# Splitting shared weights once: the first sequence stores the two-part weights, the second loads them

## The chip, the cores and the metric

One core of a Trainium2 chip runs the whole program. The metric is the time of one execution on the device in microseconds (us), lower is better. The engines named below are PE (matrix products), DVE and ACT (elementwise work), POOL, and SP, which here only issues transfers between main memory and the on-chip buffers.

## The reference

Two independent sequences, `prompt` and `sample`, of 1024 tokens by 1024 features, pass through the same encoder layer with the same weights. Cut to its core:

```python
h = rmsnorm(x, norm_g) * (1 + scale) + shift            # scale, shift, gate from the conditioning vector
a_b, a_c, a_x, a_z, q, k, v, b_z, lr_f, lr_b, m_a, m_b = split(h @ w_in)
y_a = (a_b * depthwise_conv(a_c * a_x) * silu(a_z)) @ w_a_out
o   = gated_linear_attention(q, k, v, forward) + gated_linear_attention(q, k, v, backward)
y_b = (rmsnorm_heads(o) * silu(b_z)) @ w_b_out
merged = sigmoid(m_a) * y_a + sigmoid(m_b) * y_b
y = rmsnorm(x + gate * (merged @ w_out), final_norm_g)
```

All arithmetic is float32. A product of two float32 matrices is made on PE as three products of parts: each operand is split into a rounded `hi` (an ACT cast) and a remainder `lo` (a DVE subtraction), and hi·hi, hi·lo and lo·hi are summed.

## The kernel before

The weight matrices lie in main memory as 112 tiles of 128 by 1024 floats (512 KB each). The program goes once through the stages for sequence 0 and then through the same stages for sequence 1: `projections` (most of `h @ w_in`), `mixers` (attention of four heads, one after the other, with products of the remaining projections and of `w_a_out` laid between its steps), and `merge` (`w_b_out`, `merged`). A `final` stage makes the product with `w_out` for both.

There are two kinds of products. The projections use a scheme of seven products for a 2 by 2 block of tiles (`fast`, `stationary`). Their weight operands are already made in parts only once: sequence 0 writes them to `kept_d` (L190) and sequence 1 loads them from there (`loaded`, L226 and L231). The other kind are the plain products, which take one weight tile through `load_w` (L126): two transfers of 256 KB bring the halves of a tile into `raw` buffers (L117), ACT makes `hi` (L122), DVE makes `lo` (L123), both into a `w` buffer. There are 6 `raw` buffers and 4 `w` buffers (`NW`), so the `w` buffers hold two tiles. A plain tile of weights takes 48 matmuls of 512 columns: 8 slices of the features, two halves of the tokens, three products of parts.

From weight tile `W_Q` (32) to the last of `W_B` (87) each sequence takes 28 tiles through `load_w`: in `mixers`, `gates` takes 4 of `W_Q` and `W_K` and 8 of `W_MA`; `first_out` takes 8 of `W_A`; `merge` takes 8 of `W_B`. The last two tiles of `gates`, the first two and the last two of `first_out` go as a pair through `group` (L340), which holds all four `w` buffers and four accumulators; the others go one at a time through `halves` (L328). `mixers` draws dense steps from these two generators after each step of the attention: the loop keeps a debt `owed`, to which each attention step adds 20 dense steps per head in proportion to its length.

While the last pair of `gates` runs, `reload` (L1053) brings the convolution's output in from `ta_d` for `first_out`: 16 transfers through the same 6 `raw` buffers, each split on ACT and DVE into the operand `b`. The results of that pair are taken out of the accumulators by ACT (`sg`, L764). The attention's levels copy keys on ACT (`km`, L931), multiply on PE (L903) and update Q and K on DVE (L944, L947).

[...]

Of the kernel before, what the change touches and what calls it, by code (L numbers as in the profile page):

```python
# [11 lines left out]
F32 = mybir.dt.float32  # L12
F32R = mybir.dt.float32r
# [4 lines left out]
P = 128  # L18
# [4 lines left out]
HALF = 512  # L23
# [9 lines left out]
W_AB, W_AC, W_AX, W_AZ, W_Q, W_K, W_V, W_BZ, W_MA, W_MB, W_A, W_B, W_ADA, W_GATE = (  # L33
    0, 8, 16, 24, 32, 36, 40, 48, 56, 64, 72, 80, 88, 104)
NTILES = 112
NBIG, NSMALL, NW, NRAW = 18, 6, 4, 6
# [21 lines left out]
def encoder_kernel(ctx, tc, x_p, x_s, x_t, weights, w_lr, w_gate, w_out, vectors, b_gate, final_norm_g, masks, y_p, y_s):  # L58
    nc = tc.nc
# [5 lines left out]
    sb = ctx.enter_context(tc.tile_pool(name="sb", bufs=1))  # L65
# [3 lines left out]
    dram = ctx.enter_context(tc.tile_pool(name="dram", bufs=1, space=bass.MemoryType.DRAM))  # L69
# [30 lines left out]
    mk = const.tile([P, len(MASKED), P], U8, name="mk")  # L100

    q_d, k_d, v_d, z_d, t_d = ([dram.tile([NH, P, 2, L], F32, name=f"{n}_d{s}") for s in range(2)] for n in "qkvzt")
    kept_d = dram.tile([36, 7, P, 2 * HALF], F32, name="kept_d")
    g_d = [dram.tile([2 * KT, P, L], F32, name=f"g_d{s}") for s in range(2)]
    m1_d = [dram.tile([KT, P, L], F32, name=f"m1_d{s}") for s in range(2)]
# [8 lines left out]
    def staged(src, queue=lambda load: None):  # L114

        raw = sb.tile([P, HALF], F32, name="raw", tag="raw", bufs=NRAW)
        queue(nc.sync.dma_start(out=raw, in_=src))  # L117
        return raw

    def split(hi, lo, raw, engine):  # L120

        high = nc.scalar.copy(out=hi, in_=raw)  # L122
        engine.tensor_sub(out=lo, in0=raw, in1=hi.bitcast(F32))  # L123
        return high

    def load_w(i, w=None, **kw):  # L126

        with tc.high_priority(offset=30):
            parts = []
            raws = [staged(weights[i][:, half * HALF:(half + 1) * HALF], **kw) for half in range(2)]  # L130
            for half, raw in enumerate(raws):
                t = sb.tile([P, 2, 4, P], F32R, name="w", tag="w", bufs=NW) if w is None else w[:, half]
                split(t[:, 0], t[:, 1], raw.rearrange("p (k c) -> p k c", c=P), nc.vector)
                parts.append(t)
        return lambda k: (parts[k // 4][:, 0, k % 4, :], parts[k // 4][:, 1, k % 4, :])

    def product(out, terms, first=True, last=True):
# [190 lines left out]
    def halves(i, use, act, w=None):  # L328

        w = w or load_w(i)  # L330
        for t in range(2):
            sl = slice(t * HALF, (t + 1) * HALF)
            ps = dense_ps()
            for ks in (range(KT // 2), range(KT // 2, KT)):
                mm3(ps, w, lambda k: act(k, sl), ks=ks, first=(ks[0] == 0), last=(ks[0] > 0))
                if ks[0]:
                    use(ps, sl)
                yield

    def group(items, act):  # L340


        ws = [load_w(i) for i, _ in items]
        pss = [[dense_ps(), dense_ps()] for _ in items]
        for k in range(KT):
            for w, ps in zip(ws, pss):
                for t in range(2):
                    mm3(ps[t], w, lambda k: act(k, slice(t * HALF, (t + 1) * HALF)), ks=[k], first=(k == 0), last=(k == KT - 1))
            yield
        for (_, use), ps in zip(items, pss):  # L350
            for t in range(2):
                use(ps[t], slice(t * HALF, (t + 1) * HALF))
# [63 lines left out]
    def start(mv):  # L416
# [51 lines left out]
        def weights_of(i):  # L468
            first.append(load_w((W_AC, W_AX, W_AZ)[i], w=big("wf", F32R, (P, 2, 2, 4, P)) if i == 2 else None, queue=queue))
# [748 lines left out]
```

## Time and profile before

| | |
|---|---|
| runs of the kernel | 2373.42 us median of 3 (2373.26 to 2377.82) |
| profiled execution, its own time | 2377.87 us |
| profiled execution, span of the trace | 2376.0 us |
| mean granted clock of PE | 0.987 |
| busy: PE, DVE, ACT | 2301.9, 1424.6, 1008.8 us |

The profiled execution's time is 1.87 us above its span and 4.45 us above the median of the runs. Sequence 0 has its mixers from about 666 to 1060 us and its merge to 1167; sequence 1 has its projections from 1167 to 1727, its mixers to 2110 and its merge to 2195.

### The profile page before, as it was taken

To read this page: it belongs to the slowest core of one execution; us is meant where nothing else is said; L and a number is where in the kernel's file an instruction comes from. 1 tells how busy PE (TensorE), PEld (TensorE's weight loads), DVE (VectorE), ACT (ScalarE), POOL (GpSimd) and SP (SyncE) were. 2 spreads that over 40 slices of the span, in tenths; PEclk is the share of its full clock that TensorE was granted. 3 is DMA by queue.
4 is the path that set the end of the run, shared out by engine and by line. 5 is a ranking of instruction groups with operands and counts; after the bars stand their busy time and mean duration, and the time that the engine had idled before them with its cause. 6 is when DMAs were issued, how large, how long until landed. Compare 5 with 4: busy or idle time off the path is not lost.

```text
span 2376.0 us, 29248 instructions
## 1 busy us (share of the span) xinstructions
PE 2301.9 (97%) x10897; PEld 1883.3 (79%) x10897; DVE 1424.6 (60%) x2021; ACT 1008.8 (42%) x1655; POOL 34.3 (1%) x72
## 2 busy tenths in 40 slices
PE   7999999999999989999999999999999989999998
PEld 3688887887888868878788888888778878888887
DVE  4676676666576878868622332344476876965443
ACT  4443443666655546443421112555145544442221
POOL 0000000000000000000000000000000000000000
PEclk8999999999999999999999999999999999999999
DMA  6267767888863245557366667787853244478431
GB/s 234 71 245 282 268 252 279 314 298 302 308 235 110 99 146 201 211 184 245 113 202 212 212 201 230 256 277 269 306 187 113 101 150 169 160 246 300 154 124 62
DMA packets 189902, 494.63 MB, mean 208 GB/s; under 512 B 18912, under 2 KB 45632, under 8 KB 185664
## 3 DMA queue, kind: packets, MB, share of 16 engines
q1 hardware_dynamic: 166960, 405.98, 49.8%
q10 hardware_dynamic: 22800, 86.78, 9.4%
q8 instruction: 86, 1.41, 0.2%
q14 instruction: 56, 0.46, 0.1%
HBM read 294.90 MB, written 197.79 MB: 207 GB/s over the span
## 4 chain that ended last, share of the span: by engine, by line
PE 83%; DMA 7%; DVE 6%; ACT 2%; issue 1%; POOL 1%; SPq 0%; POOLq 0%; DVEq 0%; ACTq 0%
PE ps L141 9%; PE ps L143 9%; PE ps L142 9%; PE pl L277 8%; PE pl L278 8%; PE pl L279 8%; PE ps L278 6%; PE ps L279 6%; PE ps L277 6%; PE pl L903 3%; DMA raw<-in_weights_dram 2%; DMA qk<-q_d 2%; PE pm L141 1%; PE pm L142 1%; PE pm L143 1%
## 5 line engine op out<-in xcount | busy, mean ns | idle before, releaser
L123 DVE TENSOR_TENSOR w<-raw,w 128x512 fp32r<-128x512 f32 x298 | 202.2, 686 | 100.1 <-ACT w L122 99.1
L122 ACT CAST w<-raw 128x512 fp32r<-128x512 f32 x298 | 183.3, 621 | 161.7 <-PE ps L143 51.5
L277 PE MATMUL pl<-th,w 128*128 128x512 f32 x584 | 228.1, 391 | 1.1 <-ACT keep L282 1.1
L278 PE MATMUL pl<-tl,w 128*128 128x512 f32 x584 | 227.9, 390 | 0.0
L279 PE MATMUL pl<-th,w 128*128 128x512 f32 x584 | 227.6, 390 | 0.0
L141 PE MATMUL ps<-b,w 128*128 128x512 f32 x512 | 202.8, 396 | 0.4 <-ACT w L122 0.3
L142 PE MATMUL ps<-b,w 128*128 128x512 f32 x512 | 201.8, 394 | 0.2 <-DVE b L123 0.2
L143 PE MATMUL ps<-b,w 128*128 128x512 f32 x512 | 201.0, 393 | 0.0
L141 PE MATMUL ps<-hi,w 128*128 128x512 f32 x432 | 173.5, 402 | 1.7 <-ACT hi L390 1.7
L143 PE MATMUL ps<-hi,w 128*128 128x512 f32 x432 | 171.2, 397 | 1.5 <-DVE w L123 1.5
L142 PE MATMUL ps<-lo,w 128*128 128x512 f32 x432 | 170.7, 395 | 0.7 <-DVE lo L391 0.7
L282 ACT COPY keep<-pl 128x512 f32<-128x512 f32 x116 | 67.7, 584 | 242.2 <-PE pl L279 242.1
L278 PE MATMUL ps<-lo,w 128*128 128x512 f32 x352 | 138.2, 393 | 0.4 <-DVE lo L123 0.4
L279 PE MATMUL ps<-hi,w 128*128 128x512 f32 x352 | 137.8, 391 | 0.4 <-DVE w L123 0.4
L277 PE MATMUL ps<-hi,w 128*128 128x512 f32 x352 | 137.7, 391 | 0.3 <-ACT hi L122 0.3
L277 PEld LDWEIGHTS pl<-th,w 128*128 128x128 f32 x584 | 110.0, 188 | 24.9 <-ACT keep L282 1.7
L278 PEld LDWEIGHTS pl<-tl,w 128*128 128x128 f32 x584 | 109.9, 188 | 23.0
L279 PEld LDWEIGHTS pl<-th,w 128*128 128x128 f32 x584 | 109.8, 188 | 22.9
L903 PE MATMUL pl<-Q,km 128*128 128x128 f32 x768 | 101.8, 287 | 19.4 <-ACT km L931 14.5
L903 PEld LDWEIGHTS pl<-Q,km 128*128 128x128 f32 x768 | 95.3, 198 | 31.5 <-ACT km L931 20.1
L141 PEld LDWEIGHTS ps<-b,w 128*128 128x128 f32 x512 | 97.0, 189 | 19.3 <-ACT w L122 0.7
L142 PEld LDWEIGHTS ps<-b,w 128*128 128x128 f32 x512 | 96.9, 189 | 19.0 <-DVE b L123 1.0
(287 smaller groups left out, 5043.7 us busy)
## 6 DMA issues: line engine op xcount, KB each, us to landing
kept_d<-w SPq DMA_DIRECT2D x196, 512.0 KB, 4.1
raw<-in_weights_dram SPq DMA_DIRECT2D x256, 256.0 KB, 4.3
w<-kept_d SPq DMA_DIRECT2D x112, 512.0 KB, 3.4
wk<-kept_d SPq DMA_DIRECT2D x168, 256.0 KB, 3.1
g<-g_d SPq DMA_DIRECT2D x32, 512.0 KB, 4.6
araw<-in_weights_dram SPq DMA_DIRECT2D x16, 512.0 KB, 3.7
ta_d<-u ACTq DMA_DIRECT2D x16, 512.0 KB, 3.5
v_d<-single ACTq DMA_DIRECT2D x16, 512.0 KB, 5.2
```

What stands on the lines that cost most here:

```text
L122: high = nc.scalar.copy(out=hi, in_=raw)
L123: engine.tensor_sub(out=lo, in0=raw, in1=hi.bitcast(F32))
L141: nc.tensor.matmul(out, ahi, bhi, start=(first and i == 0), stop=False)
L142: nc.tensor.matmul(out, ahi, blo, start=False, stop=False)
L143: nc.tensor.matmul(out, alo, bhi, start=False, stop=(last and i == n - 1))
L277: nc.tensor.matmul(ps, whi[:, cs], mhi, start=(first and k == 0), stop=False, skip_group_check=True)
L278: nc.tensor.matmul(ps, whi[:, cs], mlo, start=False, stop=False, skip_group_check=True)
L279: nc.tensor.matmul(ps, wlo[:, cs], mhi, start=False, stop=(k == 3), skip_group_check=True)
L282: nc.scalar.copy(out=job[i, "keep"], in_=ps)
L903: nc.tensor.matmul(pl[:, j * P:(j + 1) * P], km[:, c * P:(c + 1) * P], qm(c), start=True, stop=True)
```

## The change

For every tile from `W_Q` on, the first sequence's `load_w` also writes each half, split into its two parts, to a new memory tensor `plain_d` (512 KB per half), and notes it in `kept_w`. The second sequence's `load_w` finds the tile there and loads both halves straight into `w` buffers, without `raw`, without the cast and without the subtraction. This branch stands ahead of the `high_priority` block.

```diff
+    plain_d = dram.tile([W_ADA - W_Q, 2, P, 2 * HALF], F32, name="plain_d")
+    kept_w = {}
     kept_d = dram.tile([36, 7, P, 2 * HALF], F32, name="kept_d")
...
     def load_w(i, w=None, **kw):
 
+        if i in kept_w:
+            parts = []
+            for half in range(2):
+                t = sb.tile([P, 2, 4, P], F32R, name="w", tag="w", bufs=NW)
+                nc.sync.dma_start(out=t.bitcast(F32).rearrange("p a k c -> p (a k c)"), in_=kept_w[i][half])
+                parts.append(t)
+            return lambda k: (parts[k // 4][:, 0, k % 4, :], parts[k // 4][:, 1, k % 4, :])
         with tc.high_priority(offset=30):
             parts = []
             raws = [staged(weights[i][:, half * HALF:(half + 1) * HALF], **kw) for half in range(2)]
@@ -132,6 +141,11 @@
                 t = sb.tile([P, 2, 4, P], F32R, name="w", tag="w", bufs=NW) if w is None else w[:, half]
                 split(t[:, 0], t[:, 1], raw.rearrange("p (k c) -> p k c", c=P), nc.vector)
                 parts.append(t)
+                if i >= W_Q:
+
+                    nc.sync.dma_start(out=plain_d[i - W_Q, half], in_=t.bitcast(F32).rearrange("p a k c -> p (a k c)"))
+            if i >= W_Q:
+                kept_w[i] = plain_d[i - W_Q]
```

## Rows read from the trace of the kernel before

**Rows 1.** Page, costliest groups: form, xcount | busy us, mean ns | idle before.
```profile
L123 DVE TENSOR_TENSOR w<-raw,w 128x512 fp32r<-128x512 f32 x298 | 202.2, 686 | 100.1 <-ACT w L122 99.1
L122 ACT CAST w<-raw 128x512 fp32r<-128x512 f32 x298 | 183.3, 621 | 161.7 <-PE ps L143 51.5
```
**Rows 2.** Windows by stage: length, busy and count of each engine, clock, DMA share, GB/s.
```profile
111.00:666.00 555.00, 548.51 (x2401) 450.48 (x2400) 360.67 (x493) 284.97 (x410) 0.00 (x0) 0.99 0.77 281
666.00:1060.00 394.00, 371.25 (x2049) 313.12 (x2048) 301.88 (x462) 201.61 (x403) 9.64 (x16) 0.98 0.46 161
1060.00:1167.00 107.00, 105.08 (x451) 84.98 (x449) 81.98 (x111) 45.53 (x60) 0.00 (x0) 0.98 0.60 203
1167.00:1727.00 560.00, 553.46 (x2430) 454.84 (x2429) 197.07 (x227) 178.65 (x216) 0.00 (x0) 1.00 0.70 236
1727.00:2110.00 383.00, 367.44 (x2041) 308.92 (x2039) 292.74 (x447) 189.09 (x381) 9.68 (x16) 0.99 0.42 151
2110.00:2195.00 85.00, 83.99 (x374) 69.41 (x375) 46.16 (x65) 23.15 (x34) 0.00 (x0) 1.00 0.87 296
```
**Rows 3.** PE's waits in sequence 1's mixers (1727 to 2110): us, times, longest.
```profile
PE pl L903 <- ACT km L931: 6.7, 3, 5.0
PE pm L1046 <- DVE ot L1038: 3.3, 7, 0.5
PE pl L370 <- ACT Xh L122: 2.7, 2, 2.5
PE pl L903 <- ACT w L122: 2.1, 1, 2.1
PE ps L141 <- ACT w L122: 0.3, 1, 0.3
```
**Rows 4.** Timeline of PE, 1942 to 1960: start, us, instruction, [idle before].
```profile
1942.44 0.39 PE L143 MATMUL ps<-hi,w 128*128 128x512 f32 x1
1944.06 2.05 PE L903 MATMUL pl<-Q,km 128*128 128x128 f32 x16 [1.24 <-ACT km L931]
1951.10 3.78 PE L903 MATMUL pl<-Q,km 128*128 128x128 f32 x16 [4.99 <-ACT km L931]
1957.01 2.02 PE L903 MATMUL pl<-Q,km 128*128 128x128 f32 x16 [2.12 <-ACT w L122]
1959.16 0.50 PE L141 MATMUL ps<-b,w 128*128 128x512 f32 x1
```
**Rows 5.** Timeline of ACT, 1955 to 1960.
```profile
1955.32 1.04 ACT L931 COPY km<-K 128x1024 f32<-128x1024 f32 x1
1956.26 0.61 ACT L122 CAST w<-raw 128x512 fp32r<-128x512 f32 x1
1957.99 0.62 ACT L122 CAST w<-raw 128x512 fp32r<-128x512 f32 x1 [1.12 <-DMA raw<-in_weights_dram]
1958.52 1.56 ACT L764 ACTIVATE sg<-ps 128x512 f32<-128x512 f32 x3
```
**Rows 6.** Timeline of DVE, the update of Q before the third level's matmuls.
```profile
1955.65 1.21 DVE L944 TENSOR_TENSOR Q<-Q,T 128x1024 f32<-128x1024 f32 x1
```
**Rows 7.** Windows of 4 us: before and inside that stretch, and of sequence 0's.
```profile
1936.00:1940.00 4.00, 4.00 (x27) 3.59 (x26) 4.00 (x7) 1.80 (x3) 0.00 (x0) 1.00 0.21 62
1948.00:1952.00 4.00, 0.90 (x4) 0.90 (x5) 4.00 (x8) 2.32 (x4) 0.00 (x0) 0.58 0.24 86
...
896.00:900.00 4.00, 4.00 (x20) 3.30 (x19) 2.75 (x5) 1.05 (x1) 0.00 (x0) 1.00 1.05 436
```
**Rows 8.** Page, DMA issues: xcount, KB each, median us from issue to landing.
```profile
kept_d<-w SPq DMA_DIRECT2D x196, 512.0 KB, 4.1
raw<-in_weights_dram SPq DMA_DIRECT2D x256, 256.0 KB, 4.3
w<-kept_d SPq DMA_DIRECT2D x112, 512.0 KB, 3.4
```
**Rows 9.** SP's own waits over the whole span, first of the list: us, times, longest.
```profile
SPq L117 <- DVE w L123: 462.3, 96, 20.1
SPq L190 <- DVE w L123: 209.7, 109, 20.1
```
**Rows 10.** Chain that ended last, 860 to 990 (sequence 0): start, us, link.
```profile
900.17 6.53 DMA raw<-in_x_t_dram
932.94 4.24 DMA raw<-in_x_t_dram
```

## Prediction

> **What bounds the kernel now.** I read the windows by stage first [rows 2]. In each stage PE is busy for 94% to 99% of the time, DVE for 35% to 77%. Busy time alone can mislead, since matmuls overlap, so I checked it by count: in sequence 1's merge 374 matmuls fill 85.00 us, one every 0.227 us, and nothing but new work could make that stage shorter. PE sets the end. The change takes no matmul away, so it can only give back time in which PE stands idle, and only where splitting a weight is what PE waits for. That time is small: in sequence 1's mixers 383.00 − 367.44 = 15.6 us, in its merge 1.0 us, and its projections take no tile through `load_w`. For the 15.6 us I read PE's waits there [rows 3]; they add up to 15.1 us, and only 2.1 + 0.3 = 2.4 us name the cast of a weight. Most of the rest lies in one place, at about 1943 to 1959 us, so I read the timelines of PE, ACT and DVE there [rows 4 to 6].
>
> **That place.** The last matmul of the second pair of gate tiles starts at 1942.44; the next dense matmul, the first with a tile of W_A, starts at 1959.16. Between them stand three batches of the attention's level products, with 1.24, 4.99 and 2.12 us of idleness before them [rows 4]. [...] Everything that PE loses here is 1.24 + 4.99 + 2.12 + 1.73 + 0.3 (the wait for the second W_A tile [rows 3]) = 10.4 us. This is the prize if W_A's loads were what PE waited for.
>
> I do not think they are. DVE is busy without a gap there (4.00 of 4.00 us in 1948 to 1952 [rows 7]), with level updates and with splits of `b`; it reaches the splits of W_A only afterwards. The third batch starts at 1957.01, just after DVE's update of Q ends at 1955.65 + 1.21 = 1956.86 [rows 4, 6]. The cast named as releaser ends at 1956.26 + 0.61 = 1956.87 [rows 5], a tie, so taking it away gives nothing. The first dense matmul then needs an accumulator, which ACT's `sg` frees at about 1958.52 + 0.52 = 1959.04, and it starts at 1959.16, right behind the third batch (1957.01 + 2.02 = 1959.03). In ACT's fixed order `sg` stands behind the third `km` copy, as it does in the written order, where the debt `owed` reaches W_A's first step only after that level. The change moves neither.
>
> **The change part by part.**
>
> *Splits removed.* 28 tiles × 2 halves = 56 casts of 621 ns and 56 subtractions of 686 ns [rows 1], 34.8 us of ACT and 38.4 us of DVE, all in sequence 1's mixers and merge. PE covers them: it is 96% and 99% busy there. At the place above I count 0.3 us for the second W_A tile and 0.1 us for `sg`: 0.4. Elsewhere shorter queues on DVE and ACT could shorten the waits for `ot` and `Xh`, 3.3 + 2.7 = 6.0 us at most [rows 3]. The first is a chain through POOL of some 0.5 us each time, in which no weight stands, so I take 0.5. Gain 0.9, bounds 0 and 10.4 + 6.0 = 16.4.
>
> *Raw loads removed, two-part loads added in sequence 1.* 56 transfers of 256 KB become 56 of 512 KB, 14.7 MB more. The nearest row, `w<-kept_d`, lands in 3.4 us, less than the 4.3 us of a raw load [rows 8]. A tile needs two of the four buffers. With `halves` its loads can start when the tile before last is done, a whole tile (48 × 0.227 = 10.9 us) before it is needed, also without the 30 places of priority, since the buffer and not the order is what they wait for. Cover gone (a pair after a pair): the second tile gets its last buffers at the end of the pair before, and its first matmul comes 6 × 0.227 = 1.4 us later, so it is 3.4 − 1.4 = 2.0 us late. This occurs where the pair of W_A follows the pair of gates, and there PE starts W_A 16 us later anyway. I take 0, bounds 0 and 2.0. In the merge, DMA is the busiest (0.87 share, 296 GB/s [rows 2]); 16 loads add 16 × 0.26 = 4.2 MB in 85 us, 49 GB/s. The sum, 345 GB/s, is below the 436 GB/s seen in 896 to 900 [rows 7]. I take 0.
>
> *Stores added in sequence 0.* 56 stores of 512 KB, 29.4 MB. Each waits on SP for the subtraction of its own half. Behind it queue the next raw loads, attention's loads and `g`. But the raw loads already wait for the same subtraction, which frees their buffer: 462.3 us in 96 waits [rows 9]. So SP stands no longer than before. The stores of `kept_d` behave so too (109 waits [rows 9]) and land in 4.1 us [rows 8], and with 196 of them the projections of sequence 0 keep PE busy for 548.51 of 555.00 us, 98.8%, as against 553.46 of 560.00, 98.8%, in sequence 1, which has none [rows 2]. A `w` buffer is held until its store has read it, 4.1 us after the split; its matmuls hold it for 10.9 us. What is left is traffic. After the pair of W_A in sequence 0 the engines are full (1.05 share [rows 7]), and a load of `x_t`, on which ACT waits in order, lies on the chain for 6.53 us [rows 10]. The pair's four stores, 2.1 MB, take 2.1 MB / 436 GB/s = 4.8 us there. PE has 96 matmuls (22 us) of that pair to do meanwhile, so I take 1.0, bounds 0 and 4.8.
>
> *Sum.* −0.9 + 0 + 1.0 = +0.1 us on the profiled execution's 2377.87 (span 2376.0 and 1.87 around it): 2378.0. That execution stands 4.45 us above the median of the runs, so the forecast for the median is 2373.5 us, no change.
>
> [...]
>
> **The rivals.** A change within 4.75 us (0.2%) is about what these measurements cannot tell from none.
>
> 1. *The hole at 1943 to 1959 closes.* [...] For it: W_A's raw loads are late there (ACT idles 1.12 us for one [rows 5]). Against it: `sg` in ACT's order, and DVE full with `b`. It decides when `sg` comes ahead of the last casts of `b`. Price up to 10.4: 2373.5 − 10.4 = 2363.1.
> 2. *Stores delay the loads that sequence 0 waits for.* The load of `x_t` lands 4.8 us later, ACT holds the next `km` copy, PE idles and restarts at the lower clock (1.7 us, as in [rows 4]). It decides when PE's 22 us of W_A are spent before ACT moves on. For it: the chain goes through two such loads [rows 10]. Against: PE's cover. 2373.5 + 4.8 + 1.7 = 2380.0.
> 3. *The order on SP.* In sequence 1 a load of `w` now waits on SP for PE to free a buffer, with the next head's T, q and k behind it; each of four heads could start late by what the worst `Xh` wait shows, 2.5 us [rows 3]. 2373.5 + 10 = 2383.5. Against: raw loads hold SP in the same way today, up to 20.1 us [rows 9].
>
> **How the numbers follow.** No change 0.54, the hole closes 0.24, stores 0.17, SP's order 0.05. So faster 0.24, same 0.54, slower 0.22. The likeliest time is 2373.5, its own range ±4 for the residues above. The range for 8 in 10 goes from 2364.5, which leaves out the case that nearly all of the hole closes (about 0.1), to 2381, which leaves out rival 3 and the worst of rival 2 (about 0.08).
>
> **What would show it.** In the changed trace: 242 casts and subtractions `w<-raw` instead of 298; 56 stores `plain_d<-w` and 56 loads `w<-plain_d`, landing in about 4.1 and 3.4 us; DVE's busy time down by some 38 us, ACT's by some 35, PE's not; in sequence 1's mixers the gap between the last gate pair and W_A's first matmul still some 16 us; in sequence 0's mixers PE's idle time as before (22.8 us). I am wrong if that gap is gone, or if PE waits appear behind `x_t`, or behind `w<-plain_d`.

## The result and the profile after

The changed kernel takes 2388.37 us (median of 4 runs, 2387.04 to 2395.49) where the kernel before takes 2375.53 beside it (4 runs, 2373.26 to 2377.82). The ratio is 1.0059, 95% interval 1.0044 to 1.0073: slower by 14.0 us (10 to 17), where 2373.5 and at most 2381 were forecast. Below, every ratio is also given in us of a kernel of 2378 us. The kernel before alone spread from 2371 to 2383 us over the runs of this study, so one profile shows a wait of some us at its place but can't show a sum of 2 or 3 us; sums come from the ratios.

The page of the changed kernel: splits (form, xcount | busy us, mean ns | idle before) and DMA issues (xcount, KB each, us to landing).

```profile
L125 DVE TENSOR_TENSOR w<-raw,w 128x512 fp32r<-128x512 f32 x242 | 164.1, 687 | 96.5 <-ACT w L124 95.6
L124 ACT CAST w<-raw 128x512 fp32r<-128x512 f32 x242 | 148.6, 622 | 130.7 <-PE ps L157 24.6
...
raw<-in_weights_dram SPq DMA_DIRECT2D x200, 256.0 KB, 4.7
...
plain_d<-w SPq DMA_DIRECT2D x56, 512.0 KB, 4.2
w<-plain_d SPq DMA_DIRECT2D x56, 512.0 KB, 4.2
```

The change does what it says: 56 casts and 56 subtractions fewer than in [rows 1], 34.7 us less of ACT and 38.1 of DVE in these groups, 56 stores and 56 loads more. The loads land in 4.2 us, not in the 3.4 of `w<-kept_d` [rows 8], and a raw load now takes 4.7 instead of 4.3.

The windows by stage of the changed kernel, in the order of [rows 2]:

```profile
111.00:668.00 557.00, 550.06 (x2402) 452.13 (x2401) 360.83 (x493) 286.19 (x410) 0.00 (x0) 0.99 0.77 281
668.00:1066.00 398.00, 373.62 (x2053) 314.66 (x2052) 301.58 (x461) 197.84 (x401) 10.41 (x16) 0.97 0.59 214
1066.00:1176.00 110.00, 103.36 (x446) 83.41 (x445) 82.56 (x111) 45.19 (x60) 0.00 (x0) 0.97 0.71 257
1176.00:1736.00 560.00, 552.93 (x2428) 454.93 (x2426) 197.98 (x227) 177.50 (x214) 0.00 (x0) 1.00 0.71 239
1736.00:2118.00 382.00, 365.10 (x2029) 307.19 (x2027) 266.37 (x402) 165.58 (x339) 9.84 (x16) 0.98 0.51 173
2118.00:2203.00 85.00, 83.58 (x369) 68.19 (x369) 37.90 (x51) 14.96 (x20) 0.00 (x0) 1.00 0.95 340
```

Against [rows 2] the mixers of sequence 0 are 4 us longer and its merge 3 us; in sequence 1, where the splits are gone (DVE 292.74 to 266.37, ACT 189.09 to 165.58 in the mixers), the mixers are 1 us shorter and the merge as long as before; the stages not named differ by 2 us or less. The profit is one microsecond at most, and the loss is mainly where the stores are. Summed over the waits that the two traces list, PE waits 75.1 us where it waited 66.2: 2.3 more in 650 to 700 us, 4.8 more in 1075 to 1175, 2.5 more in 1700 to 1790 (the start of sequence 1's mixers), and about as much as before in the rest. Two single waits stand out, in the first two of these stretches; both are for a split weight, and both follow loads that came late.

The first is at the start of sequence 0's mixers. The timeline of the changed kernel there, SP's queue (SPq), ACT and PE:

```profile
661.69 0.70 SPq L902 DMA_DIRECT2D T<-t_d  x1
662.63 2.06 SPq L146 DMA_DIRECT2D plain_d<-w  x2
664.78 0.95 SPq L904 DMA_DIRECT2D qk<-q_d  x1
665.79 0.77 SPq L905 DMA_DIRECT2D qk<-k_d  x1
667.00 7.38 SPq L119 DMA_DIRECT2D raw<-in_weights_dram  x3
677.54 1.06 ACT L906 ACTIVATE qk<-qk 128x1024 f32<-128x1024 f32 x1 [9.64 <-DMA qk<-q_d]
679.64 0.80 PE L155 MATMUL ps<-hi,w 128*128 128x512 f32 x1 [3.00 <-ACT w L124]
```

The same place before:

```profile
662.46 0.43 SPq L888 DMA_DIRECT2D T<-t_d  x1
663.00 0.44 SPq L890 DMA_DIRECT2D qk<-q_d  x1
674.33 1.06 ACT L892 ACTIVATE qk<-qk 128x1024 f32<-128x1024 f32 x1 [5.64 <-DMA qk<-q_d]
```

Two stores of 512 KB stand on SP between head 0's T and its q. From the issue of T to the end of ACT's wait for q (called T to q below) it takes 677.54 − 661.69 = 15.9 us; before, 674.33 − 662.46 = 11.9. Of these 4 us, 2.6 pass before q is issued (3.09 us after T, before 0.54), while SP issues the two stores; the other 1.4 are a longer way from q's issue to ACT (12.76 us, before 11.33). Behind `qk` on ACT stand three casts of weights (at 678.97 us), and PE waits 3.00 us for one of them. Before, the largest wait there was 1.46 us. The clock adds to it: in 676 to 692 us PE's granted clock is 0.89, before 1.00, and from 680.23 to 682.36 us its matmuls start 0.43 us apart instead of 0.23.

The second is in sequence 0's merge and at its join with the projections of sequence 1. The chain that ended last, in the changed kernel, has loads of 6.5 to 9.0 us where a raw load usually lands in 4.3 [rows 8]:

```profile
1089.85 6.54 DMA raw<-in_weights_dram
...
1113.57 0.41 SPq L146
1114.04 7.41 DMA raw<-in_weights_dram
1121.53 0.63 ACT w L124
1122.18 0.70 DVE w L125
1122.90 0.33 SPq L146
1123.28 0.43 SPq L1084
1123.80 0.71 SPq L1085
1124.56 9.01 DMA raw<-in_weights_dram
1133.66 0.63 ACT w L124
```

It reads: SP issues a store (L146), behind it a raw load, the load takes 7.41 us, its split is stored, and behind that store, `g` and `m` goes the raw load of the projections' first job, 9.01 us more. The median of the 20 raw loads from 1060 to 1176 us is 6.2 us, before (1060 to 1167) 4.4. PE then waits 6.48 us (0.45 before) and restarts with matmuls 0.43 us apart instead of 0.23, at a granted clock of 0.50 in 1150 to 1152:

```profile
1149.88 0.79 PE L293 MATMUL ps<-hi,w 128*128 128x512 f32 x1 [6.48 <-DVE w L125]
```

There is a third place, without a net loss in this trace: the end of sequence 0's mixers. PE's waits in 1005 to 1075 us, before:

```profile
PE pm L1046 <- DVE ot L1038: 3.2, 2, 2.5
```

In the changed kernel, the two largest:

```profile
PE pm L1060 <- DVE ot L1052: 3.9, 2, 3.3
PE pm L155 <- ACT ot L1047: 1.8, 2, 1.0
```

They sum to 6.1 us, 2.9 more than before. Between the last steps of head 3's attention there are fewer dense matmuls to cover them: 41 with a weight in 1020 to 1055 us, before 61. In exchange PE waits less earlier in the same stage (14.3 us in 700 to 1005, before 17.8).

### The profile page after: what moved, and what is told of

Same layout as the page of the kernel before. It is cut to its first block, busy times and chain, and to the rows that moved or that the text cites. A ratio compares the mean times of both kernels' runs of the same rounds, so it can differ in the third digit from the quotient of the medians.

```text
span 2386.0 us, 29138 instructions
## 1 busy us (share of the span) xinstructions
PE 2303.3 (97%) x10897; PEld 1883.7 (79%) x10897; DVE 1393.2 (58%) x1965; ACT 975.5 (41%) x1599; POOL 35.2 (1%) x72
## 4 chain that ended last, share of the span: by engine, by line
PE 81%; DMA 7%; DVE 6%; ACT 3%; issue 1%; POOL 1%; SPq 0%; DVEq 0%; POOLq 0%; ACTq 0%
PE ps L155 9%; PE ps L157 8%; PE ps L156 8%; PE pl L291 8%; PE pl L292 8%; PE pl L293 8%; PE ps L293 6%; PE ps L292 6%; PE ps L291 6%; PE pl L917 4%; DMA raw<-in_weights_dram 3%; DMA qk<-q_d 2%; PE pm L155 1%; PE pm L156 1%; PE pm L157 1%
## 5 line engine op out<-in xcount | busy, mean ns | idle before, releaser
L125 DVE TENSOR_TENSOR w<-raw,w 128x512 fp32r<-128x512 f32 x242 | 164.1, 687 | 96.5 <-ACT w L124 95.6
L124 ACT CAST w<-raw 128x512 fp32r<-128x512 f32 x242 | 148.6, 622 | 130.7 <-PE ps L157 24.6
L917 PE MATMUL pl<-Q,km 128*128 128x128 f32 x768 | 102.5, 289 | 18.5 <-ACT km L945 15.2
```

What stands on the lines that cost most here:

```text
L917: nc.tensor.matmul(pl[:, j * P:(j + 1) * P], km[:, c * P:(c + 1) * P], qm(c), start=True, stop=True)
```

## The experiments

Fourteen kernels. The first four ask what costs the time, the next four where, the last six whether the places are understood. The engines' orders differ between the kernels too (the first stores of the changed kernel stand on SP behind head 0's T, the small stores below ahead of it), so the kernels differ in more than their edit, and no run holds the order fixed. All sums at a glance (ratio to the kernel before in the same comparison, interval, us):

| what of the change it has | ratio | interval | us |
|---|---|---|---|
| the whole change | 1.0059 | 1.0044 to 1.0073 | +14.0 |
| stores alone | 1.0041 | 1.0028 to 1.0055 | +9.8 |
| loads alone | 1.0015 | 1.0004 to 1.0026 | +3.6 |
| stores of 64 KB alone | 1.0018 | 1.0008 to 1.0029 | +4.3 |
| whole, stores issued by POOL | 1.0107 | 1.0082 to 1.0131 | +25.4 |
| W_MA and W_A | 0.9992 | 0.9982 to 1.0003 | −1.9 |
| W_B | 1.0033 | 1.0022 to 1.0044 | +7.8 |
| W_Q and W_K | 1.0039 | 1.0024 to 1.0053 | +9.3 |
| whole, first stores later | 1.0040 | 1.0027 to 1.0053 | +9.5 |
| W_MA, W_A, six tiles of W_B | 1.0033 | 1.0020 to 1.0046 | +7.8 |
| W_Q and W_K, stores later | 1.0016 | 1.0007 to 1.0026 | +3.8 |
| first stores later, last two of W_B out | 1.0028 | 1.0016 to 1.0040 | +6.7 |
| W_B's stores | 1.0021 | 1.0010 to 1.0033 | +5.0 |
| W_B's loads | 1.0011 | 1.0002 to 1.0020 | +2.6 |
| last two tiles of W_B | 1.0012 | 1.0002 to 1.0023 | +2.9 |

**Stores alone.** Sequence 0 stores, sequence 1 splits as before.

```diff
-        if i in kept_w:
+        if False:
...
-                if i >= W_Q:
+                if i >= W_Q and i not in kept_w:
```

> Sequence 0 stores the two-part weights as in the change; sequence 1 does not load them and splits raw weights as before. Theory S (the whole loss is made by the stores in sequence 0, in the three places at 662 to 690, 1020 to 1055 and 1117 to 1150 us): 10 to 12 us above before, with PE's waits of about 3 us at 680 and 6 us at 1150 there again. Rival L (the loads in sequence 1 carry half of it): at most 6 us above before.

Measured +9.8 us, just under what theory S gave and clear of rival L. Both waits are there: 3.7 us for the cast at the start of the mixers, 5.2 us for the split weight at the join. In the third place, 1005 to 1075 us, PE waits 6.6 us (3.2 before).

**Loads alone.** Nothing is stored; sequence 1 takes the operands from the memory of `kept_d`.

```diff
-                if i >= W_Q:
+                if False:
...
-                kept_w[i] = plain_d[i - W_Q]
+                kept_w[i] = [kept_d[(2 * (i - W_Q) + half) // 7, (2 * (i - W_Q) + half) % 7] for half in range(2)]
```

> No stores in sequence 0; sequence 1 loads its w operands, as many and as large, from operands of the projections that lie in kept_d, so the weights are not the right ones. Theory S: no slower than before, 0 to 3 us faster, since the gap before W_A in sequence 1 shrinks by some 2 us. Rival L: 4 to 6 us slower than before, with PE late at the start of sequence 1's mixers.

Measured +3.6 us, between the two. The loads are not free either, though their interval (1 to 6) reaches near nothing. With the stores alone they make 13.4 of the 14.0. In this trace the one stretch where PE waits over 2 us more than before is 1700 to 1790 us, the start of sequence 1's mixers (9.6 us, before 6.5), as rival L had it; in sequence 1's merge (2105 to 2210) it waits 1.7, before 1.2.

**Small stores.** As the stores alone, each cut to 64 KB of 512.

```diff
-                    nc.sync.dma_start(out=plain_d[i - W_Q, half], in_=t.bitcast(F32).rearrange("p a k c -> p (a k c)"))
+                    nc.sync.dma_start(out=plain_d[i - W_Q, half][:, :P], in_=t.bitcast(F32)[:, 0, 0, :])
```

> As e1_stores_only, but each store writes one eighth of its bytes (64 KB, the first slice of hi), behind the same wait on SP. If SP's wait and place in its queue cost the time (theory S1): 8 to 12 us above before, as with whole stores. If the traffic of the stores costs it (theory S2): 0 to 3 us above before. In between, both in proportion.

Measured +4.3 us, between theory S1 and theory S2. At the mixers' start T to q is 676.26 − 665.18 = 11.1 us and at the join PE waits 0.4 us: neither place loses. Both waits are gone with the bytes. But the order on SP is not the same: the two small stores now stand ahead of T, not between T and q, and in the merge the last raw loads stand one by one between the stores, not six behind the last store. This run alone does not part the bytes from the order. The 4.3 us that are left show in part in its trace: PE's waits sum to 69.8 us (66.2 before), with 7.7 us in 1005 to 1075 (3.2 before) against 14.9 in 700 to 1005 (17.8 before). So the third place shows here without most of the stores' bytes.

**Stores by POOL.** The whole change, with `nc.gpsimd.dma_start` for the stores.

> The whole change, with the 56 stores issued by POOL instead of SP. Theory S1 (SP's queue): about as fast as before or 0 to 3 us faster, since SP no longer holds raw loads and attention's loads behind a store. Theory S2 (traffic): 8 to 12 us above before, as the bytes are the same.

Measured +25.4 us. The page of this kernel:

```profile
plain_d<-w POOLq DMA_DIRECT2D x56, 512.0 KB, 6.4
```

The stores land in 6.4 us instead of 4.2, and T to q is 676.79 − 662.90 = 13.9 us, two less than behind SP's stores and two more than before. POOL also has the attention's scales (`ors`), which now stand behind stores that wait there for a split (41 waits, 914.9 us). Which of the two makes the 25 us was not separated, so this run decides nothing between SP's queue and traffic.

**By weight.** The next three divide the tiles: `W_MA <= i < W_B` (16 tiles), `i >= W_B` (8), `W_Q <= i < W_MA` (4), in both conditions of `load_w`.

```diff
-                if i >= W_Q:
+                if W_MA <= i < W_B:
...
-            if i >= W_Q:
+            if W_MA <= i < W_B:
```

> The change for the 16 tiles of W_MA and W_A alone; W_Q, W_K and W_B are split in both sequences as before. Theory (the loss arises where stores meet loads at the joins of sequence 0: the start of its mixers, where W_Q and W_K are split, and the join of its merge and the projections of sequence 1, where W_B is split): both joins are free again, ratio 0.999 to 1.001, that is the time before within 3 us, and PE's waits at 670 to 690 us and at 1150 us are back to those of before. Rival (each store costs a share of the 9.8 us, wherever it stands, by its traffic): 32 of 56 stores, so 32/56 x 9.8 = 5.6 us slower, ratio 1.0024, with the loss in the middle of sequence 0's mixers.

Measured −1.9 us, an interval that holds zero. 32 of the 56 stores, with their loads and with the splits that they save, cost nothing in sum, and a fair share for each store (+5.6) is refuted. PE's wait at the mixers' start is 1.8 us (1.5 before), at the join 1.7. In 1005 to 1075 us it waits 6.1 us, as with the whole change. There the traces of all kernels on SP that store W_A show 5.9 to 7.7 us, those of the changed kernels that do not 3.7 to 4.7.

> The change for the 8 tiles of W_B alone. Theory (joins): the wait for the first split tiles of the projections of sequence 1 at about 1150 us comes back (6.5 us with the whole change, 0.45 before), 3 to 5 us slower, ratio 1.0013 to 1.0021; nothing lost at 660 to 690. Rival (each store its share): 16/56 x 9.8 = 2.8 us, spread over the merge, without that wait.

Measured +7.8 us, more than either theory gave. PE waits 3.58 us at the join, and in sequence 1's merge for the loads themselves. The waits of PE in this kernel, 2105 to 2210 us:

```profile
PE ps L155 <- DMA w<-plain_d: 1.5, 3, 0.7
```

> The change for the 4 tiles of W_Q and W_K alone: 8 stores and 8 loads of 56. Theory (joins): the start of the mixers of sequence 0 loses 3 to 4 us (time from the issue of the load of head 0's T to the end of ACT's wait for q 15 to 17 us, against 11.9 before), and that of sequence 1 up to 2 us: 3 to 6 us slower, ratio 1.0013 to 1.0025. Rival (each store its share): 8/56 x 9.8 = 1.4 us, ratio 1.0006.

Measured +9.3 us, more than expected too, and over 6 times a fair share of 8 stores (1.4). T to q is 680.22 − 663.10 = 17.1 us and PE waits 4.26 us for the cast. The three parts, −1.9 + 7.8 + 9.3 = 15.2, make up the whole 14.0.

**First stores later.** The whole change, with the order on SP alone changed for the first four tiles: their stores are issued after head 0's loads of T, q and k.

```diff
+    head_loads = []
+
+    def first_store(i, store):
+        if W_Q <= i < W_MA:
+            after(store, head_loads[-1])
...
-                    nc.sync.dma_start(out=plain_d[i - W_Q, half], in_=t.bitcast(F32).rearrange("p a k c -> p (a k c)"))
+                    first_store(i, nc.sync.dma_start(out=plain_d[i - W_Q, half], in_=t.bitcast(F32).rearrange("p a k c -> p (a k c)")))
...
-        nc.sync.dma_start(out=kr, in_=k_d[s][h, :, 0, :])
+        head_loads.append(nc.sync.dma_start(out=kr, in_=k_d[s][h, :, 0, :]))
```

> The whole change, but the stores of the four tiles of W_Q and W_K are put on SP behind head 0's loads of T, q and k. Theory that the place in SP's order is half of the loss at the start of sequence 0's mixers: time from the issue of T to the end of ACT's wait for q falls from 15.9 us to 13 or 14, and the kernel is 1.5 to 3 us faster than with the whole change as it is: 8 to 11 us slower than before instead of 13. Rival (traffic alone): still 15 to 16 us, 13 us slower.

The timeline of this kernel, SP's queue and ACT:

```profile
660.82 0.47 SPq L908 DMA_DIRECT2D T<-t_d  x1
661.39 0.43 SPq L910 DMA_DIRECT2D qk<-q_d  x1
662.47 0.32 SPq L911 DMA_DIRECT2D qk<-k_d  x1
663.16 1.56 SPq L152 DMA_DIRECT2D plain_d<-w  x2
...
672.78 1.06 ACT L912 ACTIVATE qk<-qk 128x1024 f32<-128x1024 f32 x1 [5.74 <-DMA qk<-q_d]
```

T to q is 672.78 − 660.82 = 12.0 us, as before, with the same bytes a moment later; PE's wait for the cast falls to 0.46 us. The order was all of q's delay, not half of it, as the theory had it. It was not all of PE's loss there: PE now waits 1.15 us for `Xh`, and its waits in 650 to 700 us sum to 2.5 (3.8 with the whole change, 1.5 before). Measured +9.5 us instead of 14.0; the two intervals overlap, so the 4.5 us between them are not sure by this pair alone. The second wait is still there (5.6 us). Behind two stores of the same queue q took 12.76 us from its issue to ACT, ahead of them 672.78 − 661.39 = 11.39, before 11.33. The larger part of the 4 us, 2.6, is that SP issued q later.

**Six tiles of W_B.** `W_MA <= i < W_B + 6`, to see whether the last tiles' stores, ahead of the projections' raw loads, make the second wait.

> The change for W_MA, W_A and the first six tiles of W_B: 44 of 56 stores; W_Q, W_K and the last two tiles of W_B are split in both sequences. Theory (at the join of the merge and the projections of sequence 1, the stores of the last tiles stand on SP ahead of the raw loads of the first job of the projections): PE's wait for a split tile at about 1145 us is gone or below 2 us, where W_B's stores alone had 3.6 and the whole change 6.5; the time is within 3 us of before, ratio 0.999 to 1.0012. Rival (the merge of sequence 0 can't carry stores anywhere): 12 of W_B's 16 stores stay, so 12/16 of the 7.8 us that W_B's stores and loads alone cost, +6, ratio 1.0025.

PE's wait at the join is 0.7 us in its trace, as the theory had it, but the time is +7.8 us, as the rival had it. The last stores can't be all of it. (The profiled execution, 2377.03 us, was the fastest of this kernel's six, so its trace shows less than the median pays.)

**W_Q and W_K, stores later.** The order of the run before last, for these four tiles alone.

> The change for W_Q and W_K alone, as in the run that cost 9.3 us, but with their stores on SP behind head 0's loads of T, q and k. Theory (SP's order): time from the issue of T to the end of ACT's wait for q is 12 us again and PE's wait for the cast of a weight at about 680 us goes; what stays is the start of the mixers of sequence 1, 1 to 3 us slower than before, ratio 1.0004 to 1.0013. Rival (traffic of the stores): 7 to 9 us slower, ratio 1.003 to 1.004.

Measured +3.8 us instead of 9.3, a little above the theory's 1 to 3 and far below the rival's 7. So some 5.5 us of the 9.3 (give or take 4, by the two intervals) were the stores' place in SP's order. For the 3.8 the loads in sequence 1 were suspected: PE's wait for `Xh` at the start of its mixers is 4.6 us with the whole change, 4.5 with the loads alone, 4.0 with W_Q and W_K, and 2.5 before. In this trace it is 2.8, and with both places mended (below) 2.4, although W_Q and W_K are loaded in both; with the first stores later it is 4.1. In 650 to 700 us PE still waits 2.8 us (1.5 before), and at the join 2.18 (0.45 before). These are parts; the 3.8 us as a whole are not placed.

**Both places mended.** The first stores later and `W_Q <= i < W_B + 6`.

> The whole change with both places mended: the stores of W_Q and W_K behind head 0's loads on SP, the last two tiles of W_B split in both sequences. Theory: sequence 0 is back to the time of before, what stays is the start of the mixers of sequence 1 (PE's wait for Xh 4 us instead of 2.5): 0 to 3 us slower than before, ratio 1.000 to 1.0013. Rival (something else that the whole change does, as its traffic of 44 MB, costs time all over): 5 us or more, ratio above 1.002.

Measured +6.7 us. The theory of two places, with the second one at the last two tiles, fails; the rival's time is met, its cause is not shown by it. Something about W_B as a whole is left, so its stores, its loads and its last tiles were run apart, each with the condition `i >= W_B` or `i >= W_B + 6` in the edits shown above.

> W_B's 16 stores in sequence 0 alone; sequence 1 splits W_B as before. Theory (the stores are what W_B costs): 5 to 8 us slower, ratio 1.002 to 1.0034, and PE's wait for the split tile at about 1145 us is 3 us or more. Rival (the loads are): within 2.5 us of before, ratio below 1.001.

> W_B's 16 loads in sequence 1 alone, from the memory that holds other tiles split in two parts (so the values of this merge's product are others); nothing is stored. Theory (the stores are what W_B costs): within 2.5 us of before, ratio below 1.001. Rival (the merge of sequence 1 has no room for the loads): PE waits there for w and b, DMA's share is 0.95 to 1.0 in most of its windows; 3 to 6 us slower, ratio 1.0013 to 1.0025.

> The change for the last two tiles of W_B alone: 4 stores, 4 loads. Theory (their stores hold the raw loads of the first job of the projections): PE's wait at about 1145 us stays at 3 us or more, 2.5 to 4 us slower, ratio 1.001 to 1.0017. Rival (it is all of W_B's transfers): 4/16 of 7.8, 2 us or less, ratio below 1.0008, and no such wait.

Measured +5.0, +2.6 and +2.9 us. The first is at the lower end of what the theory gave, and the wait at the join is 2.93 us. The second lies between theory and rival: the DMA engines are as full as the rival said (0.96 in 2110 to 2195 us), but PE waits hardly longer there (1.7 us in 2105 to 2210, before 1.2). The third has the theory's time without the theory's wait. The stores cost more, the loads cost too (5.0 + 2.6 = 7.6 of the 7.8), and the last two tiles, a quarter of the transfers, cost 2.9, above a quarter share (2) but with PE's wait at the join at 0.4 us, not 3. What shows in its trace is a wait of PE for a load in sequence 1's merge, 1.84 us for `w<-plain_d` at 2169.68. What the stores of W_B do is seen in the window from 1080 to 1130 us, in the middle of sequence 0's merge (columns as in [rows 2]). Of the kernel before:

```profile
1080.00:1130.00 50.00, 50.00 (x222) 41.44 (x221) 43.66 (x59) 22.56 (x26) 0.00 (x0) 1.00 0.70 231
```

Of the changed kernel:

```profile
1080.00:1130.00 50.00, 50.00 (x222) 41.44 (x221) 37.77 (x49) 19.51 (x22) 0.00 (x0) 1.00 0.97 363
```

Of W_B's stores alone:

```profile
1080.00:1130.00 50.00, 49.01 (x216) 40.26 (x215) 40.57 (x53) 20.38 (x24) 0.00 (x0) 1.00 0.99 371
```

Of W_MA and W_A alone:

```profile
1080.00:1130.00 50.00, 50.00 (x223) 41.39 (x222) 40.11 (x53) 19.16 (x23) 0.00 (x0) 1.00 0.64 219
```

With W_B's stores the DMA engines are full (0.97, 0.99), without them they are not (0.70, 0.64), and the median raw load from 1060 to 1150 us takes 6.1 us with W_B's stores alone, 4.4 before. ACT's waits for raw weights in that stretch go with it. None is listed before; in the changed kernel:

```profile
ACT w L124 <- DMA raw<-in_weights_dram: 16.4, 4, 6.5
```

With W_B's stores alone:

```profile
ACT w L124 <- DMA raw<-in_weights_dram: 13.5, 6, 5.5
```

With stores of 64 KB none is listed (share 0.79), with W_MA and W_A 0.4 us. With W_B's stores alone PE waits 0.99 us for a split weight at 1093.41 and 2.93 us at 1144.24, 3.9 us beside the measured 5.0. That profiled execution (2379.62 us) is one of the faster ones of its kernel, and over the whole of it the waits sum to only 1.7 us more than before. PE is still busy in nearly all of this window and pays for the late weights behind it, at the join. With the stores of all eight tiles on SP the wait at the join is 2.9 to 6.5 us. In the seven traces without whole stores in this merge it is 0.4 to 2.2, and with the stores of the first six tiles (0.7 with W_MA and W_A, 2.0 with both places mended) or of the last two (0.4) it is no longer than that. No run moves W_B's stores in SP's order, so whether the full engines alone make the raw loads late, or also their place behind the stores, is not separated here.

No version beats the kernel before. W_MA and W_A alone come nearest, with an interval that holds no change.

## Why the prediction was wrong

The step that failed is the price of the stores in sequence 0: +1.0 us, at most 4.8, where the stores alone cost 9.8. It is taken up third, in the order of the prediction.

*Splits removed* (−0.9): right in kind. 38.1 us of DVE and 34.7 of ACT go away under a busy PE, and no kernel is measurably faster for it; the part with most of them, W_MA and W_A, is −1.9 us with stores and loads included. The size is not shown, since no run takes the splits away without putting loads in their place.

*Loads in sequence 1* (0, bounds 0 and 2.0): probably too low. Loads alone are +3.6 us (1 to 6), W_B's +2.6 (0.5 to 5). One step of it was weak: the sum of 345 GB/s in sequence 1's merge was held against 436 GB/s, the best of 4-us windows. Long windows move less: the merge of the changed kernel ran at 340 GB/s and a share of 0.95, and full windows of 50 us (shares 0.97 and 0.99) moved 363 and 371 GB/s. But the wrong ceiling is not shown to be what cost the time: the 345 GB/s were nearly served, that merge is no longer than before (85 us), and what the trace of the loads alone shows is the start of sequence 1's mixers, where the prediction took 0 and left the doubt to its third rival.

*Stores in sequence 0* (+1.0, bounds 0 and 4.8): this step failed. Stores alone are +9.8 us. It rested on two statements; the first was true and did not decide, the second was wrong.

- "So SP stands no longer than before." The stores do wait where raw loads had waited: 195.9 us in 49 waits of L146 for the subtraction of `w`, and L119's fell from the 462.3 us of [rows 9] to 49.2. SP's waits in sequence 0's mixers and merge sum to 398.8 us (660 to 1176), before to 437.9 (660 to 1167). But what counts is not how long SP stands, it is what is issued behind the bytes. The prediction names attention's loads among what queues behind a store and gives them no price. At the mixers' start two stores got between T and q and made q 4 us late; issuing them behind q and k gave 5.5 us back with W_Q and W_K alone (9.3 to 3.8), and 4.5, which is not sure, with the whole change (14.0 to 9.5).
- "What is left is traffic", priced at the pair of W_A alone. At that pair nothing was lost: PE's idle time from 866 to 945 us was 11.7 us before and 10.3 after, and W_A's stores belong to the part that cost nothing in sum. The same question was not put to the merge of sequence 0, whose stores cost 5.0 us. The stage's mean share of 0.60 [rows 2] looked like room. The middle of the stage had little: 231 GB/s at 0.70 in 1080 to 1130 us would be full at 330, and two stores for each tile of 10.9 us of matmuls ask for 2 × 0.524 MB / 10.9 us = 96 GB/s more, 327 in all. Both are estimates; the window then moved 363 and 371 GB/s at 0.97 and 0.99, so the first is about a tenth too low.

The evidence from `kept_d`, 196 stores in projections whose PE stays 98.8% busy [rows 2], was a comparison of unlike stages: there no head's load stands behind them that PE needs at once. That this is what makes the difference is argued, not tested.

*Rival 1, the hole.* Partly true, for nearly nothing. In the changed kernel W_A's first matmul comes before the third batch of level products. The timeline of PE:

```profile
1953.04 2.05 PE L917 MATMUL pl<-Q,km 128*128 128x128 f32 x16 [0.69 <-ACT km L945]
1961.51 3.78 PE L917 MATMUL pl<-Q,km 128*128 128x128 f32 x16 [6.42 <-ACT km L945]
1965.17 0.80 PE L155 MATMUL ps<-b,w 128*128 128x512 f32 x1
...
1967.31 2.02 PE L917 MATMUL pl<-Q,km 128*128 128x128 f32 x16 [0.38 <-DVE Q L958]
```

The idleness is 0.69 + 6.42 + 0.38 = 7.5 us against 1.24 + 4.99 + 2.12 = 8.4 in [rows 4]: the third wait is filled, the second is longer. The 1.73 us that the prediction adds to these waits is 3.78 − 2.05 [rows 4]; the change did not win it: the second batch takes 3.78 us again, at a granted clock of 0.50 in 1962 to 1965.

*Rival 2, stores delay loads that sequence 0 waits for.* The right mechanism at the wrong load. It named `x_t` at 900 us, late by an estimated 4.8 us that no run shows, and that load is no longer on the chain; the loads that came late were q at 665 us and raw weights from 1090 to 1133 us. These are two places, of some 5.5 us (W_Q and W_K, order alone) and 5.0 us (W_B's stores), where the rival had one of 6.5. That its single sum of 6.5 is near to each of them is luck.

*Rival 3, SP's order in sequence 1.* The longest wait for `Xh` grew from 2.5 to 4.6 us, at the first of the heads alone, where the rival had up to 2.5 us at each of four. That SP's order makes it was not tested, and two other kernels that load W_Q and W_K show 2.8 and 2.4.

*What stays open.* The 3.8 us of W_Q and W_K with their stores out of the way have no single wait in a trace that accounts for them, the 4.3 us of the small stores are seen in part, and W_B's loads have waits of 1.5 or 1.84 us in two traces and none in the run that has them alone. Whether the parts add up is not clear: first stores later with the last two of W_B out (+6.7) is 4.9 us less than its parts' 3.8 + 7.8, about what the three intervals together leave open. How much of any sum is the new order of the engines' instructions, and not the bytes or the place of a store, was not tested.

## What to carry to other kernels

A store that waits where something else had waited was not free here (56 of them +9.8 us): look at what is issued right behind it on the same queue, and put it behind the loads that another engine waits for (here 5.5 us back of 9.3, with W_Q and W_K). Ask for DMA's room in windows of the stage where the transfer goes, not in the stage's mean, and hold the sum against what long full windows moved (here 363 and 371 GB/s over 50 us), not against the best burst of the trace (436 over 4 us). A window's GB/s divided by its share was a careful estimate of its ceiling here, 330 for a window that reached 371. Work taken from engines that are covered by PE (38.1 us of DVE, 34.7 of ACT) paid nothing that could be measured here, so any traffic that buys it must have room everywhere it goes.

## What was not expected of the hardware

With the DMA engines full (share 0.97 in 1080 to 1130 us), raw loads of 256 KB on the chain took 6.5 to 9.0 us, and their median in that merge was 6.2, instead of 4.4. The same 56 stores landed in 6.4 us (median) when POOL issued them and in 4.2 when SP did. The clock's answer to a wait was not the same each time: around PE's wait of 2.93 us at the join, with W_B's stores alone, the granted clock in 1140 to 1150 us was 0.66, with matmuls 0.43 us apart from 1144.84 to 1148.68; around one of 3.58 us at the same place, with W_B's stores and loads, it was 1.00, and stayed there up to 1162. So waits of like length were paid at different prices.
